# VectorE operands of a two-headed mixer in PSUM, masks by matmul and copies, and a new order of its steps

## The chip, the cores and the metric

One core of a Trainium2 chip runs the whole program. The metric is the device time of one execution in microseconds; of the kernel before there are three runs, 1455.69, 1456.66 and 1459.97 us, with a median of 1456.66.

## What is computed

A decoder of two layers on x (512 x 1024, fp32), each layer a mixer, a cross-attention into 256 memory tokens and a gated convolutional FFN, all with a norm in front. The change is in the mixer of layer 0, which feeds two groups of heads from one projection:

```python
h = xn @ w_in
qkv, gate, beta_logit, alpha_logit, u = split(h, ...)
qkv = silu(causal_dwconv(qkv, conv_qkv))                  # width 4
q, k = l2_normalize(q), l2_normalize(k)                   # 4 heads of 128
beta = sigmoid(beta_logit)
g = -exp(a_log) * softplus(alpha_logit + dt_bias)
o = gated_delta_rule_chunked(q, k, v, g, beta)
y_a = rms_norm(o, onorm_g) * silu(gate)
y = s5_ssm(u, ...)                                        # 32 groups of 16, 64 complex states
y = gelu(y)
y_b = y * sigmoid(y @ w_glu + b_glu)
x = x + concatenate([y_a, y_b]) @ w_out
```

The delta rule solves, in each chunk, a triangular system whose matrix is (k beta) k^T times a decay, masked to the lower triangle. The kernel works with chunks of 128.

## The kernel before

Everything runs in fp32 accuracy: a projection is three fp32r matmuls for each 128 x 128 block (`mm3`, high by high, low by high, high by low). The weights are split on the fly in `_prep` (L127 to L132): ACT casts the high part, and DVE subtracts it from the raw weight, or, for the units listed in `POOL`, ACT negates it and GpSimd (POOL) adds the raw weight in a DMA. `xh`, `xl` are the two parts of x; the norm's factor comes in after the projection, as the row `rB`.

`mixer0` (L760) has a small function for each step, and the string `MIX` lists the steps in the order in which they are issued. PE and SP follow that order; the orders of DVE, ACT and POOL come from a scheduler while the program is built. Steps that matter here, with the tile names of the profile:

- `k`, `qp`, `vp`, `gp`, `su`: one projection each (`proj_ps`, L721, tile `in`), 24 matmuls. `scaled` (L729) multiplies it by `rB` out of PSUM into SBUF (L731). `conv_silu` (L737) makes the four taps: ACT the first (L741), DVE three more (L743), ACT the Silu (L744).
- `ba`, `bt` (L819): logits of beta and the decay. On DVE there follow `exp_tiny` (L670) and `log1p_tiny` (L694), polynomials on 16 to 64 columns, up to g. `gc` (L859) sums g along a chunk by two matmuls into G (L861, L862).
- `rg`, `rk` (L869, L878): 16 to 48 columns are laid out as rows by a matmul R (L285); `ssk` (L854) sums the squares of the k heads (tile `tr`, L757) and takes `rsqrt` on DVE (L198 to L201). `rowr` (L290 on) spreads a row over the partitions.
- `dec`: exp of differences of G (ACT); `kh`, `am`: the scaled k and the matrix `At` (L899, L901), whose 32 x 32 diagonal blocks go to Zin (L905). `tri` masks the four `dec` tiles on POOL (L909).
- `i`: one step of `invert` (L942), 31 of them: forward substitution of all 32 x 32 blocks at once on DVE, a product (L949, into `Xt`) and a subtraction (L950, into X), 256 columns at most. The 32nd transposes the result (L953 to L955), and then it is laid out in block-diagonal tiles Xl, Xu (L960 to L967).
- `ea`, `eb`: the off-diagonal blocks of At, by products with the constant `mk` on POOL (L977). `ya`, `xa`, `yb`, `xb` widen the inverse from 32 to 128 by matmuls (Y, L992; Xu, L1000).
- `qk` (L932): scores of q and k, with the squares of q (`tr`) and a row.
- `sw`, `st`, `sc`, `sy`: the state-space heads, in four blocks j: weights on POOL (`ssm_weights`, L1281, tiles wbr, wbi, cre, cim, ct, st), a stationary matrix (w, L1340 to L1354), the scan on DVE with parts on POOL (L1384 to L1407), the output (`sy`, L1417 to L1421), which goes to DRAM and back (dy, so) to be turned, and is split into glh and gll (L183, L184).
- `B`: a quarter or half of a projection of the memory's keys and values, as filler.

PSUM has eight banks in one pool (`ps`). The mixer ends at about 383 us, when the first matmul of the output projection starts.

Of the kernel before, what the change touches and what calls it, by code (L numbers as in the profile page):

```python
# [45 lines left out]
k3 k1 k0 rs ba rb kc1 su0 k2 kc3 bt kc0 kc2 gc su3 rg qp3 sw0 vp1 ssk eg su1 sw1 rk kh1 st0 dec1 kh0 dec0 vp3 kh2 am1  # L46
dec2 dec3 su2 kh3 am0 am2 am3 i i vt3 i i i i sc0 i i vp0 i vp2 tri st1 sc1 i gp1 sw2 i sy0 i i i i i i i i i i i gp2
qp1 gp3 i qp2 i i i qp0 gp0 sy1 qk1 i qk0 i i qk3 vt2 i vt1 i st2 i i ea1 ea0 i ea2 i ya0 i eb2 ea3 eb1 eb3 mem kt2
ya1 eb0 ya2 qk2 sc2 xa1 B ya3 B xa0 sw3 B yb1 xa2 yb0 xa3 yb2 sy2 kt0 vt0 xb1 xb0 yb3 kt1 B xb2 B W2 B U0 U2 xb3 U1
kt3 U3 B W0 cs0 B W3 W1 co0 cw1 B co1 cs1 B cw2 st3 cs2 B B cw3 sc3 co3 co2 B B B B B B so B ld sy3 rr yo2 B yo3 B B B  # L50
B B yo1 yo0 B gu0 gu1 gu2 gu3 B B B B B B
""".split()

POOL = (3, 4, 5, 6, 8, 11, 19, 20, 21, 22, 26, 27, 28, 29, 30, 32, 34, 35)


class Net:
    def __init__(self, tc, A, ctx):
# [10 lines left out]
        self.ps = P("ps", 8, space=bass.MemoryType.PSUM)  # L69
# [3 lines left out]
        self.pool_units = ()  # L73
        self.tset = "n"
# [595 lines left out]
    def exp_tiny(self, x, n, em1=False, gate=None):  # L670
# [3 lines left out]
        xc, k, r, p = (self.tiny(n, s) for s in ("ex", "ek", "er", "ep"))  # L674
# [85 lines left out]
    def mixer0(self, N, kv_out, x):  # L760
# [181 lines left out]
        def invert():  # L942
            Zt = self.zp.tile([128, 32, 32], F32, tag="z", name=self.nm("Zt"))
# [186 lines left out]
        def ld():  # L1130
# [5 lines left out]
            k=k, kc=kc, rs=rs, rb=rb, ba=ba_, bt=bt_, vp=vp, gp=gp, qp=qp, ssk=ssk, gc=gc, rg=rg, eg=eg, rk=rk, dec=dec, kh=khat, am=amat, tri=tri,  # L1136
# [10 lines left out]
    def ssm_params(self, gate):  # L1147
# [31 lines left out]
        z, sn, cs = y("az", 64), y("sn", 64), y("cs", 64)  # L1179
# [12 lines left out]
        v.scalar_tensor_tensor(cs, cs, 1.0, sn, ALU.add, ALU.mult)  # L1192
        v.scalar_tensor_tensor(cm1, sn, -2.0, sn, ALU.mult, ALU.mult)
# [378 lines left out]
```

## Time and profile before

| | us |
|---|---|
| median of three runs | 1456.66 |
| the profiled execution | 1459.64 |
| its span | 1457.9 |
| PE busy | 1359.1 (93%) |
| DVE busy | 960.0 (66%) |
| ACT busy | 617.2 (42%) |
| POOL busy | 250.3 (17%) |

The profiled execution lies 3.0 us over the median, and 1.7 us of it are outside its span. The granted TensorE clock of the whole span is 0.964 of full speed. Busy shares are means over stages: in the first 383 us PE is busy much less than after them.

### The profile page before, as it was taken

Reading aid. Unit: us, or ns where it says so; the run is one execution under the profiler, and the core shown is the slowest. Engines: PE = TensorE matmul, PEld = TensorE weight load, DVE = VectorE, ACT = ScalarE, POOL = GpSimd, SP = SyncE. Lnnn points to the kernel's source line nnn. Section 1 sums busy time; section 2 is a strip of 40 time slices with the busy share of each in tenths; the row PEclk is TensorE's granted clock in tenths of the full one; section 3 lists DMA queues with packets and bytes.
Section 4 is the critical chain, followed back from the end, with each engine's and each line's share of the span. In section 5 each row is a group of like instructions: output and inputs, shape, how many; then the busy total and the mean of one; then the engine's idle time right before and its main releaser. Section 6 shows DMA issues by size and latency. Waiting matters only on the chain.

```text
span 1457.9 us, 17572 instructions
## 1 busy us (share of the span) xinstructions
PE 1359.1 (93%) x6683; PEld 1145.8 (79%) x6683; DVE 960.0 (66%) x1548; ACT 617.2 (42%) x935; POOL 250.3 (17%) x321
## 2 busy tenths in 40 slices
PE   8369986799999999999999999979999999999997
PEld 6357765798888888888888888768888888888886
DVE  8976995945665467755773675784567745764664
ACT  6317336454544354422441345564445423432442
POOL 3964554622020020000000002120020000000003
PEclk9688986999999999999999999999999999999998
DMA  8322151247442133333333334862043333323322
GB/s 241 77 65 73 65 130 29 95 102 205 127 127 67 39 116 89 100 102 92 96 101 98 90 96 126 215 157 73 29 122 96 101 89 100 101 87 101 98 65 69
DMA packets 50772, 147.68 MB, mean 101 GB/s; under 512 B 5632, under 2 KB 13952, under 8 KB 50688
## 3 DMA queue, kind: packets, MB, share of 16 engines
q1 hardware_dynamic: 40480, 127.81, 28.3%
q0 software_dynamic: 3888, 14.16, 5.5%
q10 hardware_dynamic: 6320, 4.60, 1.0%
q8 instruction: 52, 0.85, 0.2%
q14 instruction: 32, 0.26, 0.1%
HBM read 142.35 MB, written 4.19 MB: 101 GB/s over the span
## 4 chain that ended last, share of the span: by engine, by line
PE 76%; DVE 4%; DMA 2%; ACT 1%; issue 1%; POOL 0%; ACTq 0%; POOLq 0%; DVEq 0%
PE in L176 13%; PE in L178 13%; PE in L177 13%; PE op L178 8%; PE op L177 8%; PE op L176 8%; PE kp L178 1%; PE kp L176 1%; PE kp L177 1%; DMA wl<-in_wk 1%; PE sc L178 1%; PE sc L177 1%; PE sc L176 1%; PE pv L178 0%; PE pv L177 0%
## 5 line engine op out<-in xcount | busy, mean ns | idle before, releaser
L127 ACT CAST wh<-raw 128x1024 fp32r<-128x1024 f32 (+1 forms) x230 | 237.3, 1036 | 398.7 <-PE op L177 153.4
L176 PE MATMUL in<-xh,wh 128*128 128x512 f32 x992 | 393.6, 397 | 12.9 <-DVE vl L360 7.2
L178 PE MATMUL in<-xh,wl 128*128 128x512 f32 x992 | 391.0, 394 | 4.3 <-DVE wl L132 2.5
L177 PE MATMUL in<-xl,wh 128*128 128x512 f32 x992 | 391.3, 394 | 0.0
L132 DVE TENSOR_TENSOR wl<-raw,wh 128x1024 fp32r<-128x1024 f32 (+1 forms) x203 | 251.0, 1239 | 77.2 <-ACT wh L127 74.9
L176 PEld LDWEIGHTS in<-xh,wh 128*128 128x128 f32 x992 | 189.5, 191 | 52.4 <-DVE vl L360 7.4
L178 PEld LDWEIGHTS in<-xh,wl 128*128 128x128 f32 x992 | 189.1, 191 | 45.7 <-DVE wl L132 3.1
L177 PEld LDWEIGHTS in<-xl,wh 128*128 128x128 f32 x992 | 189.4, 191 | 39.8 <-DVE xl L217 1.0
L237 POOL TENSOR_TENSOR sq<-sq,sq 128x512 f32<-128x512 f32 x28 | 46.7, 1666 | 969.2 <-ACT sq L232 871.2
L455 DVE TENSOR_TENSOR x<-op,x 128x512 f32<-128x512 f32 x68 | 46.9, 691 | 153.9 <-PE op L178 153.9
L176 PE MATMUL op<-fh,wh 128*128 128x512 f32 (+1 forms) x376 | 141.4, 376 | 0.0
L178 PE MATMUL op<-fh,wl 128*128 128x512 f32 (+1 forms) x376 | 141.2, 375 | 0.0
L177 PE MATMUL op<-fl,wh 128*128 128x512 f32 (+1 forms) x376 | 141.2, 375 | 0.0
L558 DVE TENSOR_TENSOR h<-in,rB 128x512 f32<-128x512 f32 x88 | 60.2, 688 | 87.1 <-PE in L178 87.1
L177 PEld LDWEIGHTS op<-fl,wh 128*128 128x128 f32 x376 | 70.8, 188 | 12.8
L176 PEld LDWEIGHTS op<-fh,wh 128*128 128x128 f32 x376 | 70.8, 188 | 12.8
L178 PEld LDWEIGHTS op<-fh,wl 128*128 128x128 f32 x376 | 70.8, 188 | 12.8
L183 ACT CAST fh<-a 128x512 fp32r<-128x512 f32 x44 | 27.3, 621 | 110.6 <-DVE a L570 110.6
L562 ACT ACTIVATE a<-h,small 128x512 f32<-128x512 f32 x88 | 63.3, 721 | 10.5 <-DVE h L558 9.8
L564 DVE SCALAR_TENSOR_TENSOR a<-h,small,a 128x510 f32<-128x510 f32 x88 | 65.8, 749 | 2.9
L563 DVE SCALAR_TENSOR_TENSOR a<-h,small,a 128x511 f32<-128x511 f32 x88 | 65.5, 746 | 2.5 <-ACT a L562 2.5
L566 ACT ACTIVATE a<-a 128x512 f32<-128x512 f32 x44 | 27.8, 632 | 81.0 <-DVE a L564 81.0
(464 smaller groups left out, 2177.0 us busy)
## 6 DMA issues: line engine op xcount, KB each, us to landing
raw<-in_up SPq DMA_DIRECT2D x88, 512.0 KB, 3.6
raw<-in_dn SPq DMA_DIRECT2D x32, 512.0 KB, 3.6
raw<-in_w_in SPq DMA_DIRECT2D x18, 512.0 KB, 4.3
raw<-in_wk SPq DMA_DIRECT2D x16, 512.0 KB, 4.7
raw<-in_wv SPq DMA_DIRECT2D x16, 512.0 KB, 4.0
raw<-in_wq SPq DMA_DIRECT2D x16, 512.0 KB, 4.7
raw<-in_wo SPq DMA_DIRECT2D x16, 512.0 KB, 3.6
raw<-in_dn SPq DMA_DIRECT2D x16, 384.0 KB, 3.0
```

The lines of the kernel that those rows point to most:

```text
L127: nc.scalar.copy(H, raw)
L132: nc.vector.tensor_tensor(L, raw, H.bitcast(F32), ALU.subtract)
L176: mm(ps, wh, xh, start=start, stop=False)
L177: mm(ps, wh, xl, start=False, stop=False)
L178: mm(ps, wl, xh, start=False, stop=stop)
L237: eng.tensor_tensor(N["acc"], N["acc"], sq, ALU.add)
L455: nc.vector.tensor_tensor(x[m], ps, x[m], ALU.add)
L558: nc.vector.tensor_tensor(h, ps, rB, ALU.mult)
L562: nc.scalar.activation(a, h, AF.Copy, scale=cw(2))
L563: nc.vector.scalar_tensor_tensor(a[:, 1:], h[:, : T - 1], cw(1), a[:, 1:], ALU.mult, ALU.add)
L564: nc.vector.scalar_tensor_tensor(a[:, 2:], h[:, : T - 2], cw(0), a[:, 2:], ALU.mult, ALU.add)
L566: nc.scalar.activation(a, a, AF.Silu)
```

## The change

1. `column()`: short temporaries of `rsqrt`, `exp_tiny`, `log1p_tiny` and of the sine and cosine live in a PSUM tile `area` (two banks, new pool `px`) until the inverse starts, so that an instruction has one operand in PSUM.
2. `scaled` multiplies in place in PSUM; the taps and the gates' Silu read from there.
3. X of the inverse lies in PSUM, in the two banks of `area`; DVE fills it.
4. The pool `ps` has six banks in the mixer, eight after it.
5. `tri` is gone: `rowr` adds, in four more matmuls for a head, -8192 outside the triangle, so that the exponential gives 0. The masks of At become a POOL fill and two ACT copies, or one (`block`), in place of a POOL product.
6. `ssm_weights` works on 16 channels of each half of the partitions, where it worked on 32 half filled with zeros: products of 256 columns for 512, sums in two halves, four fills more.
7. `MIX` and `POOL` are new.

```diff
+k3 k0 ba rs k1 rb kc1 bt su0 k2 kc2 su3 kc3 kc0 qp3 ssk sw0 gc su1 vp1 rg eg rk dec0 dec1 kh1 sw1 vp3 dec3 kh2 st0
+dec2 am1 kh0 su2 am2 am0 kh3 sc0 vt3 am3 i i i i vp0 i st1 vp2 i i i i i i i sc1 sy0 gp1 i i gp3 i i i i sw2 qp1 vt1 i
+gp2 qp2 i i qp0 i vt2 gp0 i i i i i sy1 ea0 i i i ea1 i i qk1 st2 ea2 i qk0 eb2 i i i ea3 mem kt2 qk3 qk2 B ya0 ya1
...
-POOL = (3, 4, 5, 6, 8, 11, 19, 20, 21, 22, 26, 27, 28, 29, 30, 32, 34, 35)
+POOL = (5, 6, 8, 9, 10, 13, 14, 15, 20, 21, 22, 23, 27, 28, 29, 30, 31, 35)
...
+    def column(self, n, s="y"):
+        if self.area is None:
+            return self.tiny(n, s)
+        if self.cur + n > 1024:
+            self.cur = 0
+        self.cur += n
+        return self.area[:, self.cur - n : self.cur]
...
-        t, q, hv = (self.tiny(n, s + c) for c in "tqv")
+        t, q = (self.column(n, s + c) for c in "tq")
+        u, hv = (self.tiny(n, s + c) for c in "uv")
...
-            i.tensor_mul(t, t, hv)
-            i.scalar_tensor_tensor(q, t, -1.25 / c, t, ALU.add, ALU.mult)
+            i.tensor_mul(u, t, hv)
+            i.scalar_tensor_tensor(q, u, -1.25 / c, u, ALU.add, ALU.mult)
...
+            mm(o, self.sel[:, c : c + 1].to_broadcast([128, 128]), RT, start=True, stop=add is None)
+            if add is not None:
+                mm(o, self.identr, add, start=False, stop=True)
...
-        xc, k, r, p = (self.tiny(n, s) for s in ("ex", "ek", "er", "ep"))
+        xc, r = (self.tiny(n, s) for s in ("ex", "er"))
+        k, p = (self.column(n, s) for s in ("ek", "ep"))
...
-        s, z, p = (self.tiny(n, q) for q in ("ls", "lz", "lp"))
+        s, z = (self.tiny(n, q) for q in ("ls", "lz"))
+        p = self.column(n, "lp")
...
-    def scaled(self, ps, rB, s):
-        h = self.t(F32, s)
-        self.nc.vector.tensor_tensor(h, ps, rB, ALU.mult)
-        return h
+    def scaled(self, ps, rB):
+        self.nc.vector.tensor_tensor(ps, ps, rB, ALU.mult)
+        return ps
...
-            gs[h] = self.scaled(self.proj_ps(N), D["rB"], "gt")
-            nc.scalar.activation(gs[h], gs[h], AF.Silu)
+            gs[h] = self.t(F32, "gt")
+            nc.scalar.activation(gs[h], self.scaled(self.proj_ps(N), D["rB"]), AF.Silu)
...
+            self.area = None
+            X = self.px.tile([128, 32, 32], F32, tag="px", name=self.nm("X"))
+            v.memset(X, 0.0)
+            v.memset(X.rearrange("p t s -> p (t s)")[:, ::33], 1.0)
...
-        def mask(lev, out, h):
-            nc.gpsimd.tensor_tensor(b3(out), b3(At[h]), self.mk[:, lev : lev + 1, :].to_broadcast([128, 4, 128]), ALU.mult)
-            return out
+        def block(h, lev):
+            E = self.t(F32, "E")
+            nc.gpsimd.memset(E, 0.0)
+            w = 32 << lev
+            for b in range(0, 128, 2 * w):
+                p, q = slice(b, b + w), slice(b + w, b + 2 * w)
+                nc.scalar.copy(b3(E)[p, :, q], b3(At[h])[p, :, q])
+            return E
...
         def combo(out, a, sa, b, sb, sub):
-            t = self.t(F32, "sw")
-            g.tensor_tensor(out, a, sa, ALU.mult)
-            g.tensor_tensor(v4(t), b, sb, ALU.mult)
-            g.tensor_tensor(out, out, v4(t), ALU.subtract if sub else ALU.add)
+            t, u = (v4(self.t(F32, "sw", (128, 256)), 16) for _ in range(2))
+            g.tensor_tensor(t, a, sa, ALU.mult)
+            g.tensor_tensor(u, b, sb, ALU.mult)
+            for (o, x), (_, y) in zip(halves(t, out), halves(u, out)):
+                g.tensor_tensor(o, x, y, ALU.subtract if sub else ALU.add)
```

Where the new order moves instructions on PE, around bt and G (in_ tiles are projections: in_669 is k2, in_816 is qp3, in_945 is su1). Before, the end of k2's projection, bt and G:

```order
L177 MATMUL in_669<-xl_195,wh_316 128x512
L178 MATMUL in_669<-xh_194,wl_317 128x512
L819 MATMUL bt_704<-ident,bf_602 128x128 x4
L861 MATMUL G_784<-g,triu 128x16
L862 MATMUL G_784<-g,ones 128x16
```

And now, the end of qp3's projection, tr and G:

```order
L186 MATMUL in_816<-xl_198,wh_712 128x512
L187 MATMUL in_816<-xh_197,wl_713 128x512
L769 MATMUL tr_851<-ones,sq_807 128x1 x4
L769 MATMUL tr_851<-ones,sq_610 128x1 x4
L769 MATMUL tr_851<-ones,sq_749 128x1 x4
L769 MATMUL tr_851<-ones,sq_798 128x1 x4
L870 MATMUL G_930<-g,triu 128x16
L871 MATMUL G_930<-g,ones 128x16
L185 MATMUL in_945<-xh_159,wh_753 128x512
```

bt has moved four projections ahead of G (su0, k2, su3, qp3 now stand between them), and the square sums tr, which stood behind G, qp3 and vp1, stand directly in front of it.

On ACT, around the output of the second state-space block. Before, with a gate and two turned v tiles between the so transfers and glh:

```order
L1421 ACTIVATE sg_1946<-sy_1933 128x512
L1423 DMA dy_1948<-sg_1946 128x512
L847 ACT_TABLE_LOAD
L847 ACTIVATE gt_1930<-gt_1930 128x512
L1426 DMA so_1950<-dy_1948 32x4x128 x4
L917 ACTIVATE cv_1494<-vt_2019,beta 128x128 x4
L917 ACTIVATE cv_952<-vt_2030,beta 128x128 x4
L183 CAST glh_1955<-so_1950 128x512
L1342 COPY w_369_2046<-w_368_2041 128x512
```

And now:

```order
L1441 ACTIVATE sg_2000<-sy_1987 128x512
L1443 DMA dy_2002<-sg_2000 128x512
L1446 DMA so_2004<-dy_2002 32x4x128 x4
L192 CAST glh_2009<-so_2004 128x512
L1362 COPY w_352_2055<-w_351_2050 128x512
L1362 COPY w_354_2062<-w_353_2057 128x512
L991 COPY E_2013<-At_1346 32x4x32 x2
L242 ACTIVATE sq_2166<-mem_2162 128x256
```

Nothing stands between the transfers and glh any more, and the first copy into an E tile stands behind it.

## Rows read from the trace of the kernel before

**Rows 1.** Windows of the whole span: us, busy us of each engine, granted TensorE clock, DMA.

```profile
42.60:145.00 102.40, 64.55 (x325) 54.30 (x325) 78.58 (x134) 38.77 (x75) 66.10 (x89) 0.78 0.26 70
145.00:231.00 86.00, 64.61 (x325) 53.42 (x324) 81.77 (x125) 31.82 (x43) 52.34 (x49) 0.88 0.34 89
231.00:383.00 152.00, 138.24 (x949) 127.09 (x950) 101.36 (x214) 83.45 (x163) 48.66 (x48) 0.92 0.45 121
383.00:1457.90 1074.90, 1055.05 (x4942) 882.89 (x4940) 663.54 (x942) 434.81 (x614) 63.04 (x49) 0.99 0.33 98
```

**Rows 2.** Timeline of PE, at its stalls: start, us, line, [idle before and releaser].

```profile
41.82 0.39 PE L178 MATMUL in<-xh,wl 128*128 128x512 f32 x1
42.05 0.60 PE L819 MATMUL bt<-ident,bf 128*128 128x128 f32 x4
65.55 0.58 PE L861 MATMUL G<-g,triu 128*128 128x16 f32 x2 [22.90 <-POOL cim L1314]
...
109.07 0.48 PE L285 MATMUL R<-ident,R 128*128 128x128 f32 x1 [8.60 <-DVE R L283]
...
139.66 1.06 PE L914 MATMUL vt<-ident,cv 128*128 128x128 f32 x4
...
211.84 1.06 PE L932 MATMUL qk<-cv,cv 128*128 128x128 f32 x8
...
230.72 2.07 PE L932 MATMUL qk<-cv,cv 128*128 128x128 f32 x8 [16.53 <-ACT cv L744]
```

**Rows 3.** Timeline of DVE, 33 to 67 us: start, us, line.

```profile
45.82 0.74 DVE L743 SCALAR_TENSOR_TENSOR cv<-k,small,cv 128x511 f32<-128x511 f32 x1
46.48 0.20 DVE L678 TENSOR_SCALAR ek<-ex 128x36 f32<-128x36 f32 x1
...
54.33 0.20 DVE L702 TENSOR_SCALAR lp<-lz 128x16 f32<-128x16 f32 x1
54.57 0.48 DVE L704 SCALAR_TENSOR_TENSOR lp<-lp,lz 128x16 f32<-128x16 f32 x2
...
60.66 3.03 DVE L704 SCALAR_TENSOR_TENSOR lp<-lp,lz 128x16 f32<-128x16 f32 x3
```

**Rows 4.** POOL groups by form, 0 to 383 us.

```profile
L1296 POOL TENSOR_TENSOR sw<-bcz,bs 128x512 f32<-128x512 f32 x8 | 8.7, 1085 | 0.0
...
L977 POOL TENSOR_TENSOR E<-At,mk 128x512 f32<-128x512 f32 x4 | 5.7, 1508 | 1.8 <-DVE ssq L937 1.8
```

**Rows 5.** DVE groups by form, 145 to 218 us.

```profile
L949 DVE TENSOR_TENSOR Xt<-Zt,X 128x255 f32<-128x255 f32 x2 | 4.8, 2397 | 0.1
L1392 DVE TENSOR_TENSOR_SCAN sz<-m,sz 128x128 f32<-128x128 f32 x8 | 3.9, 532 | 0.0
...
L731 DVE TENSOR_TENSOR gt<-in,rB 128x512 f32<-128x512 f32 x3 | 2.0, 679 | 0.0
...
L1402 DVE TENSOR_TENSOR sx<-sz,ct 128x508 f32<-128x508 f32 x2 | 1.3, 669 | 0.0
...
L950 DVE TENSOR_TENSOR X<-X,Xt 128x192 f32<-128x192 f32 x2 | 0.7, 352 | 0.0
...
L949 DVE TENSOR_TENSOR Xt<-Zt,X 128x112 f32<-128x112 f32 x2 | 0.5, 258 | 0.0
```

**Rows 6.** Windows of line L949 alone, DVE busy.

```profile
145.00:218.00 73.00, 19.46 (x31) 0.95 0.36 98
```

**Rows 7.** Windows of line L950 alone, DVE busy.

```profile
145.00:218.00 73.00, 16.65 (x31) 0.95 0.36 98
```

**Rows 8.** Timeline of ACT, 232 to 243 us.

```profile
232.65 0.60 ACT L1421 ACTIVATE sg<-sy 128x512 f32<-128x512 f32 x1
...
235.32 1.76 ACTq L1426 DMA_DIRECT2D so<-dy  x4
...
242.44 1.13 ACT L183 CAST glh<-so 128x512 fp32r<-128x512 f32 x1
```

**Rows 9.** DMA issues, 210 to 260 us: KB each, median us to landing.

```profile
dy<-sg ACTq DMA_DIRECT2D x1, 256.0 KB, 2.0
```

More of the change, by code (lines that the diff above doesn't have):

```diff
@@ L45 @@
 MIX = """
[L46 to L51, printed above, removed]
+k3 k0 ba rs k1 rb kc1 bt su0 k2 kc2 su3 kc3 kc0 qp3 ssk sw0 gc su1 vp1 rg eg rk dec0 dec1 kh1 sw1 vp3 dec3 kh2 st0
+dec2 am1 kh0 su2 am2 am0 kh3 sc0 vt3 am3 i i i i vp0 i st1 vp2 i i i i i i i sc1 sy0 gp1 i i gp3 i i i i sw2 qp1 vt1 i
+gp2 qp2 i i qp0 i vt2 gp0 i i i i i sy1 ea0 i i i ea1 i i qk1 st2 ea2 i qk0 eb2 i i i ea3 mem kt2 qk3 qk2 B ya0 ya1
+sc2 eb3 eb1 ya2 eb0 ya3 B sw3 B xa0 xa1 xa3 vt0 yb0 B xa2 yb2 B kt0 xb0 yb3 xb2 kt1 B W2 yb1 sy2 U2 B U0 B xb3 W0 xb1
+kt3 U3 U1 W1 cs0 co0 W3 B cw1 B cs1 B B B co1 B B B cw2 st3 cs2 cw3 sc3 B co2 co3 B so B ld sy3 B B rr B B B B gu0 yo2
+B gu1 B B yo0 B yo1 B yo3 B B gu2 gu3
 """.split()
-POOL = (3, 4, 5, 6, 8, 11, 19, 20, 21, 22, 26, 27, 28, 29, 30, 32, 34, 35)
+POOL = (5, 6, 8, 9, 10, 13, 14, 15, 20, 21, 22, 23, 27, 28, 29, 30, 31, 35)
 class Net:
@@ L68, in __init__ @@
         self.rp = P("rp", 2)
-        self.ps = P("ps", 8, space=bass.MemoryType.PSUM)
         self.dp = P("dp", 4, space=bass.MemoryType.DRAM)
@@ L288, in rows3, with rowr @@
         return RT
-    def rowr(self, RT, cols):
+    def rowr(self, RT, cols, add=None):
         ps = self.psum("row")
+        mm = self.nc.tensor.matmul
         for j, c in enumerate(cols):
-            self.nc.tensor.matmul(ps[:, j * 128 : (j + 1) * 128], self.sel[:, c : c + 1].to_broadcast([128, 128]), RT, start=True, stop=True)
+            o = ps[:, j * 128 : (j + 1) * 128]
+            mm(o, self.sel[:, c : c + 1].to_broadcast([128, 128]), RT, start=True, stop=add is None)
+            if add is not None:
+                mm(o, self.identr, add, start=False, stop=True)
         return ps
@@ L881, in dec @@
         def dec(h):
-            ps = self.rowr(D["RG"], range(4 * h, 4 * h + 4))
+            ps = self.rowr(D["RG"], range(4 * h, 4 * h + 4), self.neg)
             d = decT[h] = self.t(F32, "dec")
@@ L1178, in ssm_params @@
         v.tensor_scalar_mul(A4, A4, 0.5)
-        z, sn, cs = y("az", 64), y("sn", 64), y("cs", 64)
+        z = y("az", 64)
+        sn, cs = (self.column(64, q) for q in ("sn", "cs"))
         v.tensor_mul(z, A4, A4)
@@ L1467, in trunk @@
     n.pool_consts()
-    with tc.tile_pool(name="mp", bufs=1) as n.mp, tc.tile_pool(name="mix", bufs=1) as n.pp:
+    psum = dict(space=bass.MemoryType.PSUM)
+    with tc.tile_pool(name="mp", bufs=1) as n.mp, tc.tile_pool(name="mix", bufs=1) as n.pp, tc.tile_pool(name="ps", bufs=6, **psum) as n.ps, tc.tile_pool(name="px", bufs=1, **psum) as n.px:
         N = n.norm_begin("g_mix", 0, quick=True)
         E = mybir.EngineType
+        n.area, n.cur = n.px.tile([128, 1024], F32, tag="px", name="area"), 0
         with tc.manual_schedule(engines={E.PE, E.SP, E.Activation, E.DVE}):
@@ L1478, in trunk @@
             pass
-    with tc.tile_pool(name="win", bufs=1) as wpool:
+    with tc.tile_pool(name="win", bufs=1) as wpool, tc.tile_pool(name="ps8", bufs=8, **psum) as n.ps:
         for l in range(2):
```

70 lines of the change are left out of this document (31 added, 39 removed).

## Prediction, before the change was run

> **What bounds the kernel now.** I read the windows first, then PE's timeline where it stands still, then what each wait was for. After 383 us PE is busy 1055 of 1075 us, and nothing there is edited [rows 1]; before, it is busy 64.6 of 102.4, 64.6 of 86.0 and 138.2 of 152.0 us, at granted clocks of 0.78, 0.88 and 0.92. All that the change can win lies in these three stretches: 37.9 + 21.4 + 13.8 = 73 us of idle PE, and what the lower clock cost there. The large stalls are three [rows 2]: 22.9 us before G, 8.6 before the second R, 16.5 before the second qk. The row names POOL as G's releaser, but G's operand is g, the end of a VectorE (DVE) chain; so all three are waits for DVE, the last through ScalarE (ACT). DVE is slow where POOL works: two steps of L704 took 0.48 us, three others, on the same 16 columns, 3.03 while POOL was in a row of products [rows 3, 4]. A 255-wide L949 took 2.4 us beside a 0.35 us step at 192 [rows 5].
>
> **A, up to the second R.** PE's new order puts two projections (su0, k2) behind bt, so bt ends two projections earlier; matmuls start 0.23 us apart [rows 2], a projection of 24 takes 5.5, and bt ends at 42.65 - 11.0 = 31.65. From there DVE's new order has 15 convolution steps, 7 scalings, one weight split and 110 narrow instructions up to g. A wide one costs 0.66 from start to start (45.82 to 46.48), the split about two: 24 x 0.66 = 15.8. A narrow one costs 0.24 in a chain [rows 3]; where two chains alternate, as in most of this stretch, I take 0.155, so 17: g at 64.6 (0.12 to 0.24 give 61 to 74). PE has four projections of its own in the meantime and stands from 53.7 until tr and G at 64.6, 11 us instead of 22.9. Behind G are left su1 and vp1, 11 us; the chain to the second R has 37 narrow instructions, a PSUM fill and two scalings, 10 to 12 us if undisturbed. It also keeps steps that read and write SBUF, which the change leaves exposed to POOL; I add 3. The second R at 84 instead of 109: **-25**. With the slow price and the old 8.6 + 3.2 us in front of the two R, 95 and -14; with the fast one 78 and -31.
>
> **B, to the end of the last At.** vt stood at 139.66 right behind it, 30.6 us after the second R. The same matmuls follow, 16 more for the decay mask (128 columns each, 0.12 apart, the price of the 128-column ones in bt: 2 us), and DVE now does the scan of j = 0 ahead of the inverse: about 4 products, 8 scans and 4 sums of 0.4 to 0.7 us [rows 5], 8 to 9 us, half of it hidden. I take **+5**, between 0 and +10; At ends at about 120.
>
> **C, the inverse, to the second qk.** From 139.66 to 230.72 are 91 us. The 62 steps kept DVE busy 19.5 + 16.7 = 36.1 us [rows 6, 7]. Undisturbed, 112 and 192 columns took 258 and 352 ns [rows 5], so 1.18 ns a column and 126 ns fixed: 2 x 5456 columns and 62 steps make 20.6. With X in PSUM no step has two SBUF inputs: 15.5 us go. DVE had 81.8 us in 145 to 231 [rows 1]; less 15.5, less the scan of 9 that moved, less about 5 for the last convolution behind the inverse, 52 are left. PE has 64.6 and some 5 of the time before 145, less 2 for the clock: 68. So PE bounds the stretch, and POOL's masks, now fills (POOL) and block copies (ACT), lie beside it. 91 becomes 68: **-23**. If half the excess stays and the old gap opens in part, -12; with full clock and no other gap, -26.
>
> **D, after it.** The new ACT order has glh directly behind the four so transfers, and the E and X copies, from which Y starts, behind glh. In the trace sg ends at 233.25; then come the write of dy (2.0 us to landing), four issues in 1.76, a landing of some 2 and glh 1.13 [rows 8, 9]: about 7 us that ACT formerly filled with other work. With the 12 block copies (some 5 us) I take **+8**. Nothing lost is the one bound; that the 13.8 us of idle PE in 231 to 383 double, +14, the other.
>
> Six PSUM banks instead of eight, and scaling in place, which holds a bank through the convolution, cost nothing in this sum, since PE stands for DVE anyway in A, and in C a bank is needed only every 5.5 us while scaling and convolution take 4 x 0.7; without that cover a projection would wait up to 2 us. Halving the state-space products and the removal of 12 mask products (1.5 us each [rows 4]) relieve POOL, which never ends a wait of PE; I count them at nothing except through DVE.
>
> No row shows DVE writing PSUM. Reading it costs nothing: L731, with a PSUM input, took 679 ns at 512 columns, L1402, without, 669 at 508 [rows 5]. I take 0 for the write too; the upper end is the slow rival below. [...]
>
> [...]
>
> **Sum.** -25 + 5 - 23 + 8 = -35. The profiled execution took 1459.64 (span 1457.9), 3.0 over the median of the runs: 1424.6 against it, **1422** against the median. The terms' ends give -66 to +3 if all fell together; the forecast's own range is -50 to -18, so 1407 to 1439.
>
> **Rivals.**
> 1. *Larger.* DVE falls clear of POOL altogether, A ends at its -31, C at -26, B and D at 0: about -57, 1400. For it: no step in PSUM is left with two SBUF inputs. Against: the weight splits (raw and wh, both SBUF) and the R chain stay, and ACT's order is plain. 0.12.
> 2. *The contention stays in part.* Moving two projections gives A its 11 us alone, C closes only the clock and half the gap, -12, B and D as above: -23 + 13 = -10, 1447. For it: instructions with both inputs in SBUF are left between those moved, and POOL, in order, keeps reading beside them. 0.15. [...]
> 3. *No change.* A at -14, B at +10, C at -12, D at +14: -2, 1455; also what comes if the new order makes PE wait for one of its six banks at every conv. 0.07.
> 4. *Slower, by the price of PSUM.* If an instruction that writes or reads PSUM while PE fills another bank takes x longer, A pays 117x, since DVE bounds it, and C 92x (62 steps, 30 others) less the 16 us by which PE is ahead. 35 us are gone at x = 0.24 us; at x = 0.35 it is 41 + 16 = 57, 22 slower: 1479. For it: no row has DVE writing there, and a chain in PSUM pays it at each step. Against: L731 reads at no price beside a busy PE. 0.11.
>
> The forecast itself has 0.55. Within 0.3% (4.4 us, about what can be told from no change) lies rival 3, and no other's centre: same 0.07; slower 0.11; faster 0.82. For the range, 0.11 above it is the slow case and about 0.04 the upper half of "no change"; below 1400 lies half of rival 1, 0.05. So 1400 to 1452.
>
> **What would show it.** A: idle before tr or G about 11 us, G near 68, the second R near 84, L704's heir at 0.24 a step with POOL busy. C: no step of the inverse over 0.45 us, the idle before the second qk under 3 us, PE busy over 90% in the 68 us before it. D: ACT idle 4 to 6 us before the second glh, and Y waiting for an E or X copy. Wrong: narrow PSUM instructions at 0.4 us or more (rival 4); steps of the inverse still at 1 to 3 us (rival 2); PE waiting for DVE to release a bank in front of a projection.

## The result and the profile after

The changed kernel took 1423.28 us (median of 4 runs, 1422.31 to 1425.08) where the one before took 1458.32 beside it (4 runs, 1455.69 to 1460.61): a ratio of 0.9762, 95% interval 0.974 to 0.9784. The prediction was 1422, with a range of 1400 to 1452. The profiled execution took 1423.21 us, its span is 1421.2 against 1457.9, so 36.7 us are gone. They are gone by the end of the mixer, at 345 us; the long rest, 1076.3 us here and 1074.7 before, takes 1.5 us more.

The windows of the changed kernel, cut at its own milestones (us, busy us of PE, PEld, DVE, ACT and POOL, granted clock, DMA share, GB/s):

```profile
30.00:66.20 36.20, 21.70 (x96) 17.61 (x94) 30.99 (x128) 13.35 (x19) 16.27 (x66) 0.84 0.51 123
66.20:87.60 21.40, 21.08 (x85) 18.29 (x85) 19.16 (x62) 5.61 (x7) 20.56 (x35) 0.71 0.41 85
87.60:122.00 34.40, 31.81 (x198) 27.86 (x199) 17.47 (x26) 26.67 (x49) 24.60 (x34) 0.90 0.42 103
122.00:196.20 74.20, 69.91 (x372) 57.29 (x370) 66.40 (x132) 42.64 (x70) 47.40 (x61) 0.94 0.44 107
196.20:345.00 148.80, 137.81 (x912) 127.24 (x911) 94.43 (x209) 79.07 (x160) 40.92 (x54) 0.89 0.47 122
345.00:1421.00 1076.00, 1055.70 (x4941) 883.18 (x4939) 664.49 (x942) 435.39 (x615) 63.87 (x49) 0.99 0.33 97
```

The 36 us in front of tr are the only stretch left with much idle PE. The waits of PE up to 350 us say the same (engine, line waited for: us in total, times, longest):

```profile
PE tr L769 <- ACT sq L761: 14.5, 1, 14.5
...
PE row L267 <- DVE r L211: 4.2, 1, 4.2
PE row L305 <- ACT RT L297: 2.6, 1, 2.6
```

What tr waits for is sq, the square of a k head on ScalarE (65.56 to 66.19 us), behind that head's taps on VectorE and its Silu, and not g. VectorE has g done only at 72.3 (L849 below), but by then tr's 32 matmuls are under way: they last 6.9 us, from 66.24 to 73.1, at a granted clock of 0.50, and G follows them without a wait.

Of the three large stalls of [rows 2] the ones before the second R (8.6) and the second qk (16.5) are gone, and the first, 22.9, is 14.5. The milestones on PE: end of the long wait 65.55 before (at G), 66.24 now (at tr, which stood at 89.62, and with two more projections, su0 and k2, done ahead of it); G itself 65.55, now 73.09; second R 109.07, now 87.64; end of the last At 139.86, now 121.94; second qk 230.72, now 196.22; first projection of the glu 363.73, now 321.18; end of the mixer (its output projection) 383.16, now 344.93.

VectorE's groups by line, 30 to 350 us (count, busy us, mean ns of one, idle before), answer to [rows 3] and [rows 5 to 7]:

```profile
L755 DVE SCALAR_TENSOR_TENSOR cv<-in,small,cv 128x511 f32<-128x511 f32 (+2 forms) x36 | 26.7, 741 | 8.6 <-ACT cv L753 8.4
L959 DVE TENSOR_TENSOR X<-X,Xt 128x31 f32<-128x31 f32 (+15 forms) x31 | 10.7, 344 | 0.6
L958 DVE TENSOR_TENSOR Xt<-Zt,X 128x31 f32<-128x31 f32 (+15 forms) x31 | 10.3, 332 | 0.6
L720 DVE SCALAR_TENSOR_TENSOR area<-area,lz 128x16 f32<-128x16 f32 x7 | 1.2, 179 | 0.1
```

L720 is what L704 was: seven steps in 1.2 us, where three of them alone took 3.03, and POOL is busy beside them too (20.56 of 21.40 us), though with products of 256 elements a partition and not 512. Beside products of 512, in the run with old masks and weights below, L720 has the same median, 182 ns. The inverse (L958 and L959) takes 21.0 us and not 36.1; its 255-wide steps are at 0.41 to 0.42 us, not 2.4. So an input in PSUM did set such a step free here, at no price that shows.

What still reads SBUF alone still waits. VectorE's timeline right behind g (start, us):

```profile
70.31 1.99 DVE L849 SCALAR_TENSOR_TENSOR g<-g,eo 128x16 f32<-128x16 f32 x1
...
74.87 0.72 DVE L290 CAST R<-Gb 128x32 fp32r<-128x32 f32 x1
...
75.67 0.72 DVE L291 TENSOR_TENSOR r<-Gb,R 128x32 f32<-128x32 f32 x1
76.32 0.17 DVE L208 TENSOR_TENSOR area<-rkG 128x16 f32<-128x16 f32 x1
76.43 0.74 DVE L292 CAST R<-r 128x32 fp32r<-128x32 f32 x1
77.09 0.16 DVE L209 TENSOR_TENSOR rsu<-area,rsv 128x16 f32<-128x16 f32 x1
```

L290 and L292 have one input, not two, and take 0.72 to 0.74 where steps with `area` (PSUM) as an input (L209) take 0.16 to 0.17. So a step with a single input in SBUF was slow here too. L208 has its inputs in SBUF as well: at 76.32 it falls between two POOL products, of which one ends at 76.35 and the next starts at 76.41. L849 (inputs in SBUF) waits for more than one product: it ends with the last of three products of 256 (70.49, 71.07, 71.65 to 72.28), although POOL's last DMA issue was at 44.52.

### The profile page after: what moved, and what is told of

It is laid out like the page before. It is cut to its first block, busy times and chain, and to the rows that moved or that the text cites. A ratio compares the mean times of both kernels' runs of the same rounds, so it can differ in the third digit from the quotient of the medians.

```text
span 1421.2 us, 17648 instructions
## 1 busy us (share of the span) xinstructions
PE 1362.0 (96%) x6699; PEld 1150.6 (81%) x6699; DVE 915.4 (64%) x1551; ACT 623.5 (44%) x951; POOL 222.6 (16%) x351
## 4 chain that ended last, share of the span: by engine, by line
PE 79%; DMA 3%; DVE 2%; ACT 2%; issue 1%; POOL 1%; ACTq 0%; POOLq 0%; SPq 0%
PE in L185 13%; PE in L187 13%; PE in L186 13%; PE op L186 9%; PE op L185 9%; PE op L187 9%; DMA raw<-in_wk 1%; PE kp L187 1%; PE kp L186 1%; PE kp L185 1%; DMA wl<-in_wk 1%; PE tr L769 1%; PE vp L185 1%; PE vp L186 1%; PE sc L187 1%
## 5 line engine op out<-in xcount | busy, mean ns | idle before, releaser
L141 DVE TENSOR_TENSOR wl<-raw,wh 128x1024 fp32r<-128x1024 f32 (+1 forms) x203 | 244.1, 1205 | 79.4 <-ACT wh L136 77.1
L578 DVE SCALAR_TENSOR_TENSOR a<-h,small,a 128x510 f32<-128x510 f32 x88 | 65.8, 749 | 2.9
```

What stands on the lines that cost most here:

```text
L141: nc.vector.tensor_tensor(L, raw, H.bitcast(F32), ALU.subtract)
L578: nc.vector.scalar_tensor_tensor(a[:, 2:], h[:, : T - 2], cw(0), a[:, 2:], ALU.mult, ALU.add)
```

## The experiments

Two theories stood first. *Contention*: the gain is VectorE's freedom from POOL's SBUF accesses, given by operands in PSUM. *Order*: the gain is the new tables MIX and POOL. Each ratio is to the kernel before, run beside it; the microseconds are medians, and between two rows that were not run beside each other they can differ by some us where the ratios do not, so the ratios decide.

| kernel | us | ratio (interval) |
|---|---|---|
| the change | 1423.3 | 0.9762 (0.974 to 0.9784) |
| before, with the new order alone | 1466.0 | 1.0043 (1.0016 to 1.0071) |
| the change in the old order | 1461.2 | 1.0014 (1.0002 to 1.0025) |
| the change, X in SBUF | 1427.4 | 0.9774 (0.9751 to 0.9797) |
| the change, short temporaries in SBUF | 1428.0 | 0.9782 (0.9761 to 0.9804) |
| the change, all three kinds of operand in SBUF | 1442.9 | 0.9913 (0.9877 to 0.9949) |
| the change, masks and 512-wide weights as before | 1450.0 | 0.9938 (0.9915 to 0.9961) |
| that, without two DMA issues of POOL | 1432.6 | 0.982 (0.9806 to 0.9833) |
| new order alone, without the two issues | 1457.0 | 0.9994 (0.9984 to 1.0005) |
| the change, masks on POOL as before | 1413.8 | 0.97 (0.9669 to 0.9732) |
| the change, the causal mask alone on POOL | 1421.2 | 0.974 (0.9723 to 0.9757) |
| the change, loads of su and so on SP's queue | 1449.4 | 0.9934 (0.991 to 0.9958) |
| masks on POOL, loads of su issued later | 1417.1 | 0.9705 (0.9688 to 0.9722) |

**The order alone.** Both tables whole, with tri, which the order of the change does not name, behind "am3 i i i i".

```diff
--- before
 MIX = """
-k3 k1 k0 rs ba rb kc1 su0 k2 kc3 bt kc0 kc2 gc su3 rg qp3 sw0 vp1 ssk eg su1 sw1 rk kh1 st0 dec1 kh0 dec0 vp3 kh2 am1
+k3 k0 ba rs k1 rb kc1 bt su0 k2 kc2 su3 kc3 kc0 qp3 ssk sw0 gc su1 vp1 rg eg rk dec0 dec1 kh1 sw1 vp3 dec3 kh2 st0
...
-POOL = (3, 4, 5, 6, 8, 11, 19, 20, 21, 22, 26, 27, 28, 29, 30, 32, 34, 35)
+POOL = (5, 6, 8, 9, 10, 13, 14, 15, 20, 21, 22, 23, 27, 28, 29, 30, 31, 35)
```

> The kernel before with the new order of steps and the new list of POOL units, the mask step put behind the fourth step of the inverse; all operands, masks and state-space weights as before. Contention theory (the gain is VectorE's steps no longer blocked by GpSimd's reads of SBUF): the blocked steps stay, so most of the 35 us does not come: 1446 us (1438 to 1458), idle PE before tr and G 20 us or more, steps of the inverse still at 1 to 3 us. Order theory (two projections and the square sums in the stall, everything else follows): 1430 us or less.

1466.0, a little slower than before, though its ten runs go from 1457.6 to 1477.7 and the profiled one is the fastest of them. PE reached bt at 30.2 us and G at 74.4, much as the change does (29.3 and 73.1), and then stood 13.7 us before the first R (102.9). VectorE's timeline there:

```profile
77.64 23.70 DVE L198 TENSOR_TENSOR rst<-rkG 128x16 f32<-128x16 f32 x1
101.26 0.16 DVE L863 COPY G<-G 128x16 f32<-128x16 f32 x1
```

One step of 16 columns, 23.70 us long. No step that long is in the profile of before. Its longest in the mixer is a weight split of 6.37 us, where a split beside no POOL work takes some 1.2 (the one at 36.33 us in the change: 1.23), and it starts right behind a DMA issue of POOL and lasts through the four products that follow (VectorE, then POOL):

```profile
115.77 6.37 DVE L132 TENSOR_TENSOR wl<-raw,wh 128x1024 fp32r<-128x1024 f32 x1 [4.04 <-ACT wh L127]
115.10 0.92 POOL L130 DMA_DIRECT2D wl<-in_w_in  x1 [7.41 <-ACT wl L129]
...
119.48 1.56 POOL L1324 TENSOR_TENSOR ct<-ct,tt 128x512 f32<-128x512 f32 x1
```

So the long form of the wait, to which the runs below come back, was in the kernel before too.

**The change in the old order.** Both tables of before, without tri.

```diff
--- the change
 MIX = """
-k3 k0 ba rs k1 rb kc1 bt su0 k2 kc2 su3 kc3 kc0 qp3 ssk sw0 gc su1 vp1 rg eg rk dec0 dec1 kh1 sw1 vp3 dec3 kh2 st0
+k3 k1 k0 rs ba rb kc1 su0 k2 kc3 bt kc0 kc2 gc su3 rg qp3 sw0 vp1 ssk eg su1 sw1 rk kh1 st0 dec1 kh0 dec0 vp3 kh2 am1
...
-POOL = (5, 6, 8, 9, 10, 13, 14, 15, 20, 21, 22, 23, 27, 28, 29, 30, 31, 35)
+POOL = (3, 4, 5, 6, 8, 11, 19, 20, 21, 22, 26, 27, 28, 29, 30, 32, 34, 35)
```

> The changed kernel with the old order of steps and the old POOL units, without the mask step on GpSimd. Contention theory: the chain to G ends some 8 us earlier and the inverse is 10 to 15 us shorter: 1437 us (1430 to 1444). Order theory: 1450 us or more.

1461.2: nothing is left of the gain. The seven steps of L720 are free here too (1.48 us), but G comes no earlier, since VectorE's order, which the builder sets, puts the polynomials for the state space weights ahead of the chain to g (the row names POOL as the releaser, as in [rows 2]; the operand is g):

```profile
PE G L870 <- POOL r16a L1257: 23.8, 1, 23.8
```

So in this order the freed time on VectorE is taken by other work. Neither theory holds alone: apart the two parts give +0.4% and +0.1%, together -2.4%.

**X in SBUF; the short temporaries in SBUF.**

```diff
--- the change
-            X = self.px.tile([128, 32, 32], F32, tag="px", name=self.nm("X"))
+            X = self.zp.tile([128, 32, 32], F32, tag="z", name=self.nm("X"))
```

> The changed kernel with the X of the inverse in SBUF again, filled by VectorE, all else as changed. Contention theory: the 62 steps take 10 to 16 us longer beside GpSimd; VectorE was busy 66 of 74 us in that stretch, so 3 to 9 us of it reach the end: 1429 us (1426 to 1433). Order theory: 1424 us, steps within 0.5 us.

```diff
--- the change
     def column(self, n, s="y"):
-        if self.area is None:
+        if True:
             return self.tiny(n, s)
```

> The changed kernel with the short temporaries of the rsqrt, exponential, logarithm and sine in SBUF again. Contention theory: the logarithm's steps that run beside GpSimd's products cost up to 0.8 us more each, G comes 4 to 8 us later: 1428 us (1425 to 1432). Order theory: 1423 to 1424 us.

1427.4 and 1428.0: by the medians some 4 to 5 us each, by the ratios 0.1 and 0.2%, and both intervals overlap that of the change, so neither loss is clear of the noise. With X in SBUF the inverse takes 30.9 us and not 21.0, and the second qk stands 7.6 us later (203.8), but what follows it runs at a granted clock of 1.00 there and not at 0.50, and Y starts at 212.4, as with X in PSUM. With the temporaries in SBUF the second R stands 4.1 us later and the last At ends at 129.9. This run moves more than operands: the scheduler that sets VectorE's order now has g done at 54.1 us, where the change has it at 72.3, and tr still starts only at 65.8. VectorE shows a second very long step, smaller than the first:

```profile
76.17 8.53 DVE L291 TENSOR_TENSOR r<-Gb,R 128x32 f32<-128x32 f32 x1
84.61 0.17 DVE L693 TENSOR_SCALAR ek<-ex 128x48 f32<-128x48 f32 x1
```

**All operands in SBUF.** The two edits above and the scaling:

```diff
--- the change
     def scaled(self, ps, rB):
-        self.nc.vector.tensor_tensor(ps, ps, rB, ALU.mult)
-        return ps
+        h = self.t(F32, "in")
+        self.nc.vector.tensor_tensor(h, ps, rB, ALU.mult)
+        return h
```

> The change with its order, masks and weights, but X, the short temporaries and the scaled projections all in SBUF. Theory 1 (what the change saves is VectorE's waiting on SBUF beside GpSimd; the order only lets that time reach the end): nearly all is lost, 1450 to 1460 us; L720's heir and the inverse steps stretch again where GpSimd is busy, and the second qk stands at 215 us or later. Theory 2 (the saving is the order together with the shorter GpSimd work; the place of the operands is worth the few us that X and the short temporaries cost when moved alone): 4.2 + 4.8 + about 2 us are lost, 1432 to 1438 us, second qk near 205 to 210 us.

1442.9 (six runs, 1440.5 to 1454.5), 19.6 us lost by the medians and 1.5% by the ratios, between the two theories. Here too VectorE's order has changed (g at 54.0). tr waits 19.6 us and not 14.5, RT 4.8 and not 2.6, a new wait of 7.0 us stands before w (for ssq, L943), and a convolution tap takes 1025 ns and not 741. One tap lasts 3.84 us (59.70), beside a run of POOL products of 256 with no issue since 45.17; and behind the issue at 81.56 three narrow steps last 5.3 to 5.5 us (85.05 to 90.6). Together the operands are worth more than X and the temporaries one at a time (4.1 and 4.8); the taps alone were not run.

**Masks and weights as before.** The new order and the operands in PSUM stay; ssm_weights and the layout of bc are those of before (products of 512 elements a partition), and the masks are products on POOL:

```diff
--- the change
-dec2 am1 kh0 su2 am2 am0 kh3 sc0 vt3 am3 i i i i vp0 i st1 vp2 i i i i i i i sc1 sy0 gp1 i i gp3 i i i i sw2 qp1 vt1 i
+dec2 am1 kh0 su2 am2 am0 kh3 sc0 vt3 am3 i i i i tri vp0 i st1 vp2 i i i i i i i sc1 sy0 gp1 i i gp3 i i i i sw2 qp1 vt1 i
-            ps = self.rowr(D["RG"], range(4 * h, 4 * h + 4), self.neg)
+            ps = self.rowr(D["RG"], range(4 * h, 4 * h + 4))
-            E0[h] = block(h, 0)
+            E0[h] = mask(0, self.t(F32, "E"), h)
-        S4 = [128, 4, 4, 16]
+        S4 = [128, 4, 4, 32]
...
```

> The change with its order and its operands in PSUM, but masks on GpSimd and 512-wide weights as before (the causal mask stands behind the fourth am and four inverse steps). Theory 1: VectorE's work in PSUM does not feel GpSimd, so little is lost, 1426 to 1434 us; the loss would be that GpSimd has some 30 us more to do and that E and the weights come later, ScalarE gets 32 copies fewer. Theory 2 (order with shorter GpSimd work): most is lost, 1445 to 1465 us, with TensorE waiting for wl, E or dec behind GpSimd between 90 and 200 us.

**The masks alone on POOL.** The same without the part on the weights.

> The change with the causal mask and the block masks E as products on GpSimd again, all else kept. Theory 1: 1423 to 1427 us, since GpSimd has room from 90 us on (its busy share there is under a half) and ScalarE loses about 32 copies in 120 to 196 us. Theory 2: 1430 to 1440 us, TensorE waits for At or E behind GpSimd's weight products, of which one channel block holds the queue for some 10 us.

1450.0 and 1413.8. So the masks of the change cost 9.5 us by the medians (0.6%; the two intervals do not touch), and its narrower weights, with the masks on POOL, are worth 36 (2.4%). Theory 2 has the first time, but not its place (TensorE does not wait for wl, E or dec), and neither theory had the second run. Up to G the two kernels are alike (73.0 and 73.2); then the first R stands at 104.73 in the one and at 87.12 in the other, 17.6 of the 36 us. VectorE in the kernel with old masks and weights:

```profile
80.59 23.64 DVE L291 TENSOR_TENSOR r<-Gb,R 128x32 f32<-128x32 f32 x1
104.15 0.17 DVE L208 TENSOR_TENSOR area<-rkG 128x16 f32<-128x16 f32 x1
```

And POOL beside it:

```profile
80.49 0.85 POOL L139 DMA_DIRECT2D wl<-in_w_in  x1
81.17 1.50 POOL L1313 TENSOR_TENSOR wbi<-wbi,sw 128x512 f32<-128x512 f32 x1
...
83.00 1.82 POOL L1313 TENSOR_TENSOR cre<-cre,sw 128x512 f32<-128x512 f32 x1
84.25 1.82 POOL L1327 TENSOR_TENSOR cim<-cim,swn 128x512 f32<-128x512 f32 x1
...
102.48 1.69 POOL L1313 TENSOR_TENSOR wbi<-wbi,sw 128x512 f32<-128x512 f32 x1
```

The reader is to see two things. From the DMA issue on, each POOL instruction begins before the one ahead of it has ended (83.00 + 1.82 is past 84.25). And the VectorE step ends at 104.2, when POOL's run ends (102.48 + 1.69). The step of 23.70 us in the first experiment has the same look: POOL's issue at 77.52, its run's last product from 99.56 to 101.29. The one of 8.53 us starts behind issues too (from 75.89), but ends at 84.7, within POOL's run, whose instructions overlap until 85.9.

**Without the two issues.** The two weight units whose issues stood there are subtracted by VectorE, in the kernel with old masks and weights and then in the one with the order alone:

```diff
-POOL = (5, 6, 8, 9, 10, 13, 14, 15, 20, 21, 22, 23, 27, 28, 29, 30, 31, 35)
+POOL = (5, 6, 8, 13, 14, 15, 20, 21, 22, 23, 27, 28, 29, 30, 31, 35)
```

> The kernel with old masks and 512-wide weights (new order, operands in PSUM), with two weight units' accumulating DMA taken off GpSimd (units 9 and 10, whose issues stood at 80.5 and 82.4 us there; VectorE subtracts them). There one VectorE step of 128x32 (L291, SBUF alone) lasted 23.64 us, from just behind GpSimd's DMA issue at 80.49 until GpSimd's run of 512-wide products ended at 104.2. Theory A (the DMA issue lets GpSimd's next instruction begin before the last has ended, and so the run holds SBUF without a break): without the issue no narrow VectorE step lasts over 3 us, the first R stands near 87 to 90 us, 1425 to 1435 us. Theory B (512-wide products one behind the other hold SBUF by themselves): a narrow step again lasts 10 to 24 us in 75 to 105 us, the first R stands behind 100 us, 1445 to 1455 us.

1432.6, 17.4 us less, as theory A had it, although VectorE has two more splits to do. The first R comes at 89.0. POOL's products are as wide and as many:

```profile
83.31 2.27 POOL L1313 TENSOR_TENSOR wbi<-wbi,sw 128x512 f32<-128x512 f32 x1
85.55 1.28 POOL L1313 TENSOR_TENSOR cre<-cre,sw 128x512 f32<-128x512 f32 x1
86.79 1.31 POOL L1327 TENSOR_TENSOR cim<-cim,swn 128x512 f32<-128x512 f32 x1
```

VectorE meanwhile:

```profile
84.44 1.19 DVE L291 TENSOR_TENSOR r<-Gb,R 128x32 f32<-128x32 f32 x1
85.55 1.31 DVE L208 TENSOR_TENSOR area<-rkG 128x16 f32<-128x16 f32 x1
...
86.90 0.17 DVE L209 TENSOR_TENSOR rsu<-area,rsv 128x16 f32<-128x16 f32 x1
86.99 1.16 DVE L293 TENSOR_TENSOR R<-r,R 128x32 fp32r<-128x32 f32 x1
```

Now each product begins where the last one ended, but for some hundredths, and a VectorE step that reads SBUF waits for one product, 1.0 to 1.3 us, and not for the whole run. L208 writes PSUM and still waits, while L209, with one input in PSUM, and L293, with both in SBUF, stand beside the same product and take 0.17 and 1.16: it is the input that counts. The short waits still cost: the second R stands at 99.5, where the kernel with narrow weights has both R by 87.5. And with the other issues left on POOL the long form stays elsewhere: behind one at 257.22 a weight split lasts 6.47 us.

> The kernel before with the new order alone (1466.0 us), with the accumulating DMA of weight units 9 and 10 taken off GpSimd as in the run before; VectorE subtracts them. There one VectorE step of 128x16 (L198) lasted 23.70 us, from behind the DMA issue at 77.52 to the end of GpSimd's run at 101.3. If that one step is what makes the order alone worth nothing: no narrow step over 4 us in 70 to 105 us, the R pair near 85 to 95 us and not 103 and 106.5, 1443 to 1452 us. If it is VectorE's many shorter waits in SBUF (the polynomials, the inverse), or the wide products by themselves: R again behind 100 us, 1460 to 1468 us.

1457.0: 9 us less than the order with the issues by the medians (0.5% by the ratios, 7 us), not the 14 to 23 that were expected. The step of 23.70 us is 1.21 here, and the first R stands at 94.5, not 102.9; but many short waits, which in the other run lay inside the long one, follow it here:

```profile
77.95 1.21 DVE L198 TENSOR_TENSOR rst<-rkG 128x16 f32<-128x16 f32 x1
...
96.09 4.72 DVE L684 SCALAR_TENSOR_TENSOR ep<-ep,er 128x48 f32<-128x48 f32 x6
```

The six steps of L684 take 1.47 us in PSUM. The second R comes at 104.3, only 2.2 us earlier than with the issues (106.5), and the inverse takes 20.1 + 20.9 us. The two profiled executions, 1455.2 and 1457.6, differ by 2.4 us; what the rest of the 9 us is lies in runs without a trace and is not shown. So the order alone loses to both forms of the wait, the long one and the short ones.

**Where the masks' 9.5 us lie.** The causal mask alone on POOL:

```diff
--- the change
-dec2 am1 kh0 su2 am2 am0 kh3 sc0 vt3 am3 i i i i vp0 i st1 vp2 i i i i i i i sc1 sy0 gp1 i i gp3 i i i i sw2 qp1 vt1 i
+dec2 am1 kh0 su2 am2 am0 kh3 sc0 vt3 am3 i i i i tri vp0 i st1 vp2 i i i i i i i sc1 sy0 gp1 i i gp3 i i i i sw2 qp1 vt1 i
-            ps = self.rowr(D["RG"], range(4 * h, 4 * h + 4), self.neg)
+            ps = self.rowr(D["RG"], range(4 * h, 4 * h + 4))
```

> The change with the causal mask of dec as a product on GpSimd again, but the block masks E still by copies on ScalarE. With both on GpSimd the time was 1413.8 us, with neither 1423.3. If the matmuls that add the mask are what costs (16 more passes on TensorE, 1.8 us, and row units that wait): 1414 to 1418 us. If the 32 copies on ScalarE cost it (ScalarE late with X, Xl and wh between 196 and 245 us): 1421 to 1424 us. If it is where the builder's order happens to fall, between the two or outside of both.

1421.2. By the medians 2.1 of the 9.5 us go with the causal mask and 7.4 with the copies of the blocks E on ScalarE (there are 12 of them, not the 32 that these expectations name); but the interval overlaps both that of the change and that of the kernel with both masks on POOL, so the split is likely and not shown. With both masks on POOL:

```profile
196.00:212.00 16.00, 13.22 (x85) 12.87 (x86) 13.86 (x38) 12.55 (x32) 1.87 (x2) 0.79 0.05 13
212.00:240.00 28.00, 20.12 (x164) 18.71 (x163) 24.45 (x62) 11.73 (x24) 18.42 (x25) 1.00 0.38 121
```

and the change in the same windows:

```profile
196.00:212.00 16.00, 16.00 (x77) 15.94 (x77) 8.40 (x21) 10.79 (x29) 0.00 (x0) 0.50 0.01 4
212.00:240.00 28.00, 19.81 (x150) 18.61 (x148) 25.75 (x70) 15.61 (x35) 15.96 (x25) 0.93 0.26 81
```

The second qk differs by 2.9 us (193.4 and 196.2), Y by 4.3, the glu by 9.8 (311.4 and 321.2). From 212 to 240 us PE is as busy in both; the change has the lower granted clock in both windows, and it waits 4.2 us before row (L267) where the other waits 1.6. That the copies bring that wait about is not shown.

**ScalarE's queue.** In the change the loads su<-du stand in ScalarE's queue right behind the store they wait for, and a convolution behind them (timeline of ScalarE):

```profile
47.41 0.35 ACTq L1385 DMA_DIRECT2D du<-sp  x1
53.67 1.99 ACTq L1388 DMA_DIRECT2D su<-du  x4
55.70 0.69 ACT L753 ACTIVATE cv<-in,small 128x512 f32<-128x512 f32 x1 [8.69 <-issue]
```

The loads wait 6.3 us, and VectorE then stands 3.8 us for that tap, on the way to g. Two tries:

```diff
--- the change
-            nc.scalar.dma_start(U[tau * 32 : tau * 32 + 32], d[:, tau, :].rearrange("(j c) n -> c j n", j=4))
+            nc.sync.dma_start(U[tau * 32 : tau * 32 + 32], d[:, tau, :].rearrange("(j c) n -> c j n", j=4))
...
-            nc.scalar.dma_start(o[j * 32 : j * 32 + 32], d[:, j, :].rearrange("(t c) n -> c t n", t=4))
+            nc.sync.dma_start(o[j * 32 : j * 32 + 32], d[:, j, :].rearrange("(t c) n -> c t n", t=4))
```

> The change with the loads su<-du and so<-dy issued from SP's queue and not from ScalarE's. If the 14.5 us that TensorE waits before tr hold 3.8 us that VectorE stands because ScalarE's queue holds the convolution's first tap behind the DMA su<-du: VectorE's idle time before L755 near 56 us falls under 1 us, tr comes 2 to 4 us earlier, the gelu before the second qk no longer stands behind so<-dy, and the time is 1417 to 1421 us. Rival: SP's queue then holds weight loads behind the same wait of about 6 us, or the chain to tr has a second wait as late (VectorE's polynomials of the state space parameters stand in the same stretch): within 2 us of the change, 1421 to 1426 us.

1449.4. The wait before tr falls from 14.5 to 5.9, though tr itself starts later, at 69.0: SP's queue, which also issues the weight loads, waits for the same stores (97.9 us for du, 87.2 for dy in all), and PE waits 20.0 us for wl. The rival, and larger than it was put.

```diff
--- the kernel with masks on POOL
-        U = self.t(F32, "su", (128, 4, 128))
-        for tau in range(4):
-            nc.scalar.dma_start(U[tau * 32 : tau * 32 + 32], d[:, tau, :].rearrange("(j c) n -> c j n", j=4))
-        return U
+        return d
...
+        def sr(j):
+            us[j] = self.ssm_ur(us[j])
...
-k3 k0 ba rs k1 rb kc1 bt su0 k2 kc2 su3 kc3 kc0 qp3 ssk sw0 gc su1 vp1 rg eg rk dec0 dec1 kh1 sw1 vp3 dec3 kh2 st0
+k3 k0 ba rs k1 rb kc1 bt su0 k2 kc2 sr0 su3 kc3 kc0 qp3 ssk sw0 gc sr3 su1 vp1 rg eg rk dec0 dec1 sr1 kh1 sw1 vp3 dec3 kh2 st0
```

> The kernel with masks on GpSimd (1413.8 us) with the loads su<-du issued from ScalarE's queue as before, but each some 20 us behind its store du<-sp, so that no convolution tap stands behind a wait for the store. If VectorE's idle 3.9 us before L756 at 56.35 us is that wait, tr starts 2.5 to 4 us earlier and the time is 1409 to 1412 us. Rival: the chain to tr holds other work as late (the polynomials and the state space parameters stand between the taps on VectorE), or what is gained is lost at the next wait, for the projections behind G: 1412.5 to 1415 us.

ssm_ur holds the four lines that ssm_u loses, and sr2 stands ahead of sc0. The wait goes: tr starts at 59.4 and not at 66.4, and the second R at 82.6, 4.5 us earlier. Then it is given back: the last At ends 1.3 us earlier, the second qk stands 1.4 us later and Y 2.8 later. The times, 1417.1 and 1413.8, cannot be told apart (ratios 0.9705 and 0.97; the profiled run, 1418.2, is the slowest of five that go down to 1413.5). Behind the inverse VectorE again shows the long form of the wait:

```profile
189.76 8.20 DVE L227 SCALAR_TENSOR_TENSOR mz<-mem,small,mz 128x256 fp32r<-128x256 f32 x4
197.88 0.68 DVE L944 TENSOR_TENSOR dec<-qk,dec 128x512 f32<-128x512 f32 x1
```

The first of the four steps is 7.01 us of it. POOL issued a DMA at 180.46, and from there to 196.5 it ran without a break, with overlapping instructions.

## Why the prediction was right

The time was right, 1423.3 for 1422, and so was the mechanism in the main: DVE's steps with an input in PSUM do run free beside POOL (L720: 179 ns, where three in SBUF took 3.03 us), and the new order brings that to the end. Of the four terms the first two are near (second R -21.4 for -25, and +3.5 for +5 to the end of At). C and D were off, 6 us too little and 10 us too good, and cancelled: that the sum came so close is luck.

- **A.** bt, two projections earlier, ended at 29.9 (31.65 was forecast). PE then stood 14.5 us and not 11, g was done at 72.3 and not 64.6, and G started at 73.1 and not near 68. Of g's delay 3.8 us are VectorE's stand behind ScalarE's loads of su (the same wait was foreseen for glh and overlooked here) and 1.8 are L849; the rest is not taken apart. The text had PE waiting for g; it waited for sq, and tr at a clock of 0.50 then covered most of g's delay. Behind G the chain took the length forecast (14.5 us to the second R, for some 16).
- **B.** +3.5; nothing to add.
- **C, -16.6 and not -23.** The steps of the inverse came as forecast (21.0 us for 20.6, none over 0.43), PE is 94% busy in the stretch (69.91 of 74.20), and no second qk waits. What failed is "PE has 64.6 and some 5": the third block's stationary matrix (st2) stands ahead of the second qk in the new order, 9.7 us at a granted clock of 0.56 with 4.3 us of waits inside and ahead of it (1.22, 2.24, 0.82). Before, it stood behind it, for 5.3 us (241.0 to 246.4).
- **D, -2 and not +8.** The loads of so do hold glh, as forecast: ScalarE is idle 5.9 us before the glh at 197.06 (4 to 6 was said). But PE has no such idle time behind the second qk, where 16.3 us of matmuls at a clock of 0.50 stand in front of Y, and Y does not wait for an E or X copy; the wait lay beside them, and st2 had gone forward. What was taken as a wait on the path was covered.
- **Halved products and masks "at nothing except through DVE".** The sum was right in that POOL ends no wait of PE, but through DVE the weights are worth 36 us, about as much as the order (37.9 when it is put back), and the masks were no relief: they cost 9.5. These worths do not add up, since each was taken with the other parts in place.
- **The cause.** The text gave 11 us of A to the two projections that moved, and the rest of A and C to the operands. Put back in SBUF one kind at a time the operands cost 0.1 and 0.2%, within the noise, all together 1.5%; and with the order put back the rest of the change gives nothing. The contention is the cause, but three parts of the change act on it: inputs in PSUM (the step takes 0.17 us and does not wait), products of half the width (the step that waits takes 0.7 us and not 1.0 to 1.3), and the order (the step that waits does so clear of POOL's DMA issue and the run behind it, and the freed time goes to the chain).
- **The ends.** "-66 to +3 if all fell together" does not follow from the terms: their ends sum to -57 and -2, as in the first and third rivals. The forecast's own range does not rest on it.
- **Rivals.** A price of a PSUM operand (0.11), put at 0.24 us and more, is not there: taps took 741 ns, as undisturbed ones in SBUF did (0.74 [rows 3]), and 112 columns of the inverse 272 to 282 ns against 258 in SBUF, 14 to 24 more. Contention that stays in part (0.15) is real, in steps like L849 (1.99 us), but small in this order; the runs in other orders show how near it was: 1450 with the old masks and weights.

The fastest kernel here is the change with the masks on POOL as before, 1413.8 us, 0.6% under the change (medians, each against the kernel before).

## What to carry to other kernels

Where VectorE is slow beside POOL, look in the timeline for the single longest step, not at means: one step of 16 columns lasted 23.7 us. What it costs is another matter: without it the kernel was 17.4 us faster in one pair of runs, and in the traces of the other pair only 2.4. Shorten POOL's instructions (a waiting step took 0.7 us beside products of 256, 1.0 to 1.3 beside 512), break its runs (L291 took 1.19 us without the two issues, 23.64 with them), or give VectorE's narrow steps an input in PSUM (0.17 us); and read each part of such a change in the order it will run in, since here neither the order alone nor all the rest without it gave anything. Look at what stands in a queue behind a DMA that waits for a store: with the loads of su in ScalarE's queue, where they waited 6.3 us, VectorE stood 3.8 us for the tap behind them, and with the loads of su and so in SP's TensorE waited 20.0 us for weights.

## What the runs showed of the hardware

- Narrow VectorE steps with all their inputs in SBUF took 0.72 to 0.74 us beside a POOL product of 256 elements a partition (L290 and L292 in the change) and 1.0 to 1.3 beside products of 512 (1.19 and 1.16 for L291 and L293 with old masks and weights, 1.04 for L281 with the order alone, both without the two issues); in the gap between two products L208 took 0.17. With one input in PSUM the step took 0.17 us beside a product of 512 (L209); with only its output there 1.31 (L208).
- Beside products of 256 a step with all its inputs in SBUF also outlasted more than one, with no DMA issue of POOL near: L849 took 1.99 us, through three of them, and a tap 3.84 us in the run with all operands in SBUF.
- In runs of POOL instructions that begin with a DMA issued by POOL such a step also lasted to the run's end (23.70, 23.64 and 7.01 us) or for a good part of it (8.53). In each of these runs POOL's instructions overlap by some tenths of a us, and without the two issues they do not, in that stretch, and the wait is one product (1.21 and 1.19 us for the first two). An issue alone was not enough: in the change (77.08 and 82.18 us) and in the fastest kernel (76.72 and 81.84) the next product begins only behind the issue's end, nothing overlaps, and no step beside them lasts over 1.3 us. So in these runs the mark of the long wait was the overlap. Why an issue brings it about in some runs and not in others stays open.
